# A decoder layer's mixer: sample columns taken with a pair's first 256, merged columns returned by DMA alone, two input tiles side by side

## The chip, the cores and the metric

The kernel runs on one core of a Trainium2 chip. The metric is the time of one execution on the device, in microseconds (us). Of three runs before the change the median is 3203.73 us, the lowest 3203.45 and the highest 3207.47. One execution was recorded by the profiler; it took 3211.86 us.

## The reference, cut to what matters

One layer works on 1024 prompt columns and 8 sample columns (each of 1024 channels), side by side in one array of NT = 1032 columns. The samples share every weight with the prompt but have states of their own.

```python
def _layer(h, ...):
    h = _layer_norm(DN_ALPHA * h + 0.5 * _swiglu(h, ...))
    mix, ... = _mixer(h, ...)
    h = _layer_norm(DN_ALPHA * h + mix)
    h = _layer_norm(DN_ALPHA * h + _xattn(h, ...))
    h = _layer_norm(DN_ALPHA * h + 0.5 * _swiglu(h, ...))

def _mixer(h, S0, shift0, h0, buf0, P):
    proj = h @ P['w_in']                      # RWKV columns, LRU, GeLU and two gates
    ...                                       # token shift, decay, keys
    S_new, y = _rwkv_scan(S0, r, decay, k, v, kk, a)
    rwkv_out = (group_norm(y) + bonus) * g
    ...                                       # causal convolution, gates, linear scan hs
    lru_out = hs * gelu(p_gelu)
    merged = gates[0] * rwkv_out + gates[1] * lru_out
    return merged @ P['w_mix_out'], ...
```

## The kernel before, in words

The layer is four stages: a feed-forward (`ffn`), the mixer, cross-attention, a second feed-forward. Activations lie transposed, 128 channels by columns, as a high and a low part (`HH`, `HL`, eight blocks of 128 channels each), and every large product is three matmuls (`mm3`, lines 125 to 127). This case is about the mixer alone, lines 543 to 1363.

In the mixer the 16 heads are eight pairs p, one for each block of 128 channels, and two pairs (p = 2g, 2g + 1) are worked together. The prompt is cut into n = 0 to 3 of 256 columns, so there are 16 units t = 4g + n. `NCW` (line 534) gives n = 3 eight columns more, the samples. The steps of a unit are Python generators:

- `stage` (line 808) loads a pair's projected columns from the DRAM tile `GD` (tiles `R` and `za`), makes keys, decays and scores, and stores the bonus. With n = 3 it also does the sample columns and keeps what the samples need in `P.sv` and `P.sg`; `samples_a` follows it.
- `inverse` (line 930) inverts 32 by 32 triangles on VectorE, 31 dependent steps over `tq` and `iv`, and sends the result through DRAM into `TT` and `TB`.
- `chain` (line 1081) carries the state over the four 64-column chunks of a unit and ends with the late steps `post` (line 1051), which normalise, gate and merge the two pairs' 256 columns into `ysb`.
- `branch` (line 985) is the linear recurrence of one pair and one n: it loads `cb` and `ge` from `GD`, works in `xc`, `gr`, `gi` and `lm`, and stores the result. With n = 3 it also does the samples' columns.
- `samples_b` (line 1153) is the samples' state update of one pair, on VectorE over tiles `ws` and `wt`; `samples_c` (line 1195) normalises and merges the samples' columns.
- `gemms` (line 660) is the stream of large products that fills TensorE: tiles of 128 output channels in three chunks of 344 columns (`CH3`), 24 matmuls a chunk, each tile's weights loaded in two halves one tile ahead (`load`, `split_half` at line 90; four halves have room). Its last tile is followed by `out_proj` (line 1238), 18 matmuls a chunk, over the merged columns of pairs 0 to 5.

Merged columns of pairs 0 to 5 go to the DRAM tile `MG` (lines 1075 and 1221). They may return into blocks 0 to 5 of `HH` and `HL` only when the last input tile has read a chunk there: `merged` (line 1226) loads 344 columns into an `ev` tile (line 1233), and `direct` (line 1046) copies them to `HH` on ScalarE and subtracts into `HL` on VectorE. The last two pairs merge into `HH` and `HL` at once, at `post`.

What sets the order: the program order gives priorities, and when the kernel is built a scheduler with estimated durations lays down each engine's own order from them; on the chip each engine follows it strictly. Loads and stores are all issued from SyncE's queue. The loop at line 1317 gives each unit its streams with a number of steps, and `rounds` (line 49) deals them out over 13 rounds, the fill by `FILL` (line 538). The streams of a unit t are:

```python
s = [(chain(units[t - 1], units[t]), 13)] if t else []
s.append((inverse(units[t]), 52))
if t + 1 < nu:
    s.append((stage_unit(t + 1), 40 if n == 2 else 34))
to = nu if t == nu - 1 else t
```

Branches up to unit `to` - 1 come next, then a pair's `samples_b` in units with n = 3 and n = 0, both pairs' `samples_c` in n = 1, and the fill. The last unit takes four branches, two `samples_b`, the rest of the fill and all late posts; the last two `samples_c` stand behind the loop (line 1338). Then the pools of the loop are given back (line 1339) and `out_last`, the first products of the next stage and the last `chain` run together.

## Time and profile before

| what | before |
|---|---|
| median of 3 runs | 3203.73 us (3203.45 to 3207.47) |
| profiled execution | 3211.86 us |
| span from the first to the last instruction | 3210.0 us |
| mean granted clock of TensorE | 0.969 |
| ScalarE (ACT) busy | 1432.5 us, 45% of the span |
| GpSimd (POOL) busy | 560.6 us, 17% |
| DMA | 386.72 MB in 381445 packets |

PE is TensorE, PEld its weight loads, DVE VectorE, SP SyncE. A granted clock of 1 stands for 2.4 GHz and 0.5 for 1.2 GHz; a mean between them is a share of time at each. The profiled execution lies 8.1 us above the median, so only differences within it are used. In the page's forty slices TensorE is at nine tenths or more through both feed-forwards; the slices around two thirds of the span, the mixer's end, are the low ones.

### The profile page before, as it was taken

What the parts mean: (1) busy time and instruction counts of PE and PEld (TensorE: products, weight loads), DVE (VectorE), ACT (ScalarE), POOL (GpSimd) and SP (SyncE); (2) the same over time, 40 slices, a digit from 0 to 9 for tenths busy, and PEclk for the clock granted to TensorE, in tenths of its full rate; (3) what the DMA queues carried; (4) which work ended last, traced back from release to release, by engine and by line L of the source; (5) the groups of instructions that cost most, each with busy time, mean ns of one, the idle gap of its engine ahead of it and who ended that gap; (6) DMA issues with size and microseconds to landing.
All of it is one profiled execution on the core that took longest, in us unless ns stands there. A gap on an engine that the chain in (4) does not pass through costs nothing. (4 is left out here: it accounts for less than half of the span.)

```text
span 3210.0 us, 63182 instructions
## 1 busy us (share of the span) xinstructions
PE 3018.8 (94%) x23324; PEld 2845.2 (89%) x23324; DVE 2202.1 (69%) x5895; ACT 1432.5 (45%) x3191; POOL 560.6 (17%) x526
## 2 busy tenths in 40 slices
PE   8999999999999999999998888789897999999997
PEld 8999999999888888888886777688887999999997
DVE  7666665574357888777877776776767666666556
ACT  5333352125565665655654554364235433334212
POOL 2222200132000101100110100350005322220111
PEclk9999999999999999999999979799999999999998
DMA  4222253314644455455544544654533222225321
GB/s 138 78 81 77 80 162 106 112 47 143 204 120 123 136 149 146 129 142 159 144 121 133 141 135 128 195 177 135 149 112 118 75 80 80 80 80 159 107 86 54
DMA packets 381445, 386.72 MB, mean 120 GB/s; under 512 B 144048, under 2 KB 282320, under 8 KB 381136
## 3 DMA queue, kind: packets, MB, share of 16 engines
q1 hardware_dynamic: 381136, 382.69, 40.1%
q8 instruction: 183, 3.00, 0.4%
q14 instruction: 126, 1.03, 0.1%
HBM read 277.54 MB, written 105.23 MB: 119 GB/s over the span
## 5 line engine op out<-in xcount | busy, mean ns | idle before, releaser
L125 PE MATMUL ps<-HH,wh 128*128 128x258 f32 (+1 forms) x2384 | 719.3, 302 | 17.0 <-ACT HH L510 7.9
L126 PE MATMUL ps<-HL,wh 128*128 128x258 f32 (+1 forms) x2384 | 717.4, 301 | 0.0
L127 PE MATMUL ps<-HH,wl 128*128 128x258 f32 (+1 forms) x2384 | 716.3, 301 | 0.0
L125 PE MATMUL g<-HH,wh 128*128 128x344 f32 (+2 forms) x1840 | 617.3, 336 | 17.3 <-ACT wh L99 6.5
L127 PE MATMUL g<-HH,wl 128*128 128x344 f32 (+2 forms) x1840 | 594.4, 325 | 3.2 <-DVE wl L100 3.1
L126 PE MATMUL g<-HL,wh 128*128 128x344 f32 (+2 forms) x1840 | 595.7, 324 | 0.3 <-POOL HL L215 0.2
L125 PEld LDWEIGHTS ps<-HH,wh 128*128 128x128 f32 x2384 | 452.1, 190 | 19.1 <-ACT HH L510 7.9
L126 PEld LDWEIGHTS ps<-HL,wh 128*128 128x128 f32 x2384 | 451.7, 189 | 0.5 <-DVE HL L511 0.4
L127 PEld LDWEIGHTS ps<-HH,wl 128*128 128x128 f32 x2384 | 451.0, 189 | 0.0
L125 PEld LDWEIGHTS g<-HH,wh 128*128 128x128 f32 x1840 | 355.2, 193 | 34.2 <-ACT wh L99 7.8
L127 PEld LDWEIGHTS g<-HH,wl 128*128 128x128 f32 x1840 | 354.1, 193 | 10.1 <-DVE wl L100 6.1
L126 PEld LDWEIGHTS g<-HL,wh 128*128 128x128 f32 x1840 | 355.8, 193 | 5.7 <-POOL HL L215 0.9
L228 ACT ACTIVATE wh<-raw 128x512 fp32r<-128x512 f32 x280 | 176.5, 631 | 321.8 <-PE ps L126 264.4
L334 POOL TENSOR_TENSOR raw<-raw 128x512 f32<-128x512 f32 x160 | 213.8, 1336 | 567.4 <-DVE wl L229 342.4
L229 DVE TENSOR_TENSOR wl<-raw,wh 128x512 fp32r<-128x512 f32 x280 | 206.5, 738 | 137.9 <-ACT wh L228 131.0
L100 DVE TENSOR_TENSOR wl<-raw,wh 128x512 fp32r<-128x512 f32 x302 | 218.7, 731 | 104.4 <-ACT wh L99 101.3
L99 ACT ACTIVATE wh<-raw 128x512 fp32r<-128x512 f32 x302 | 185.8, 627 | 219.3 <-PE ps L126 76.6
L442 DVE SCALAR_TENSOR_TENSOR acc<-ps,acc 128x344 f32<-128x344 f32 x336 | 168.9, 513 | 143.0 <-PE ps L127 142.0
L550 DVE TENSOR_TENSOR pr<-tq,iv 128x2 f32<-128x2 f32 (+30 forms) x496 | 161.0, 325 | 3.2
L555 ACT ACTIVATE ev<-g 128x344 f32<-128x344 f32 x192 | 87.3, 455 | 158.7 <-PE g L127 155.3
L945 DVE TENSOR_REDUCE tq<-pr 128x1 f32<-128x2 f32 (+30 forms) x496 | 121.9, 246 | 2.6
L374 ACT ACTIVATE g<-g 128x258 f32<-128x258 f32 x160 | 67.1, 419 | 114.0 <-DVE g L333 114.0
(410 smaller groups left out, 6364.4 us busy)
## 6 DMA issues: line engine op xcount, KB each, us to landing
raw<-in_wi_dram SPq DMA_DIRECT2D x176, 256.0 KB, 2.7
raw<-in_w_in_dram SPq DMA_DIRECT2D x116, 256.0 KB, 3.5
GD<-ev SPq DMA_DIRECT2D x168, 172.0 KB, 2.0
raw<-in_wo_dram SPq DMA_DIRECT2D x104, 256.0 KB, 3.4
raw<-HID SPq DMA_DIRECT2D x88, 258.0 KB, 3.2
HID<-g SPq DMA_DIRECT2D x80, 258.0 KB, 2.5
tg<-GD SPq DMA_DIRECT2D x32, 512.0 KB, 4.2
wt<-T SPq DMA_DIRECT2D x160, 64.0 KB, 2.7
```

Of the source, the lines that this page charges most:

```text
L99: nc.scalar.activation(out=hi, in_=raw, func=AF.Identity)
L100: S.low.tensor_tensor(out=lo, in0=raw, in1=hi.bitcast(F32), op=ALU.subtract)
L125: nc.tensor.matmul(ps, wh, xh, start=first, stop=False)
L126: nc.tensor.matmul(ps, wh, xl, start=False, stop=False)
L127: nc.tensor.matmul(ps, wl, xh, start=False, stop=last)
L228: nc.scalar.activation(out=hi, in_=x, func=AF.Identity)
L229: nc.vector.tensor_tensor(out=lo, in0=x, in1=hi.bitcast(F32), op=ALU.subtract)
L334: pool_tt = lambda o, a, b, op: nc.gpsimd.tensor_tensor(out=o, in0=a, in1=b, op=op)
L442: nc.vector.scalar_tensor_tensor(out=a, in0=q, scalar=0.5 / ALPHA, in1=a, op0=ALU.mult, op1=ALU.add)
L550: TTo = lambda o, a, b, op: nc.vector.tensor_tensor(out=o, in0=a, in1=b, op=op)
L555: ACT = lambda o, a, f=AF.Identity, **kw: nc.scalar.activation(out=o, in_=a, func=f, **kw)
L945: nc.vector.tensor_reduce(out=tq[:, 0:m, i], in_=pv, axis=mybir.AxisListType.X, op=ALU.add)
```

## The change

Sample columns move from a pair's last 256 columns (n = 3) to its first (n = 0): `stage` and `branch` load them as pieces of their own beside the 256, `samples_a` follows n = 0, `samples_b` comes in units n = 1 and 2, `samples_c` in n = 3. Branches are dealt out by halves of a unit, so that units 12 to 15 take two, three, three and two. Merged columns of pairs 0 to 5 are split into high and low part at `post` and at `samples_c`, stored into two DRAM tiles `MH` and `ML`, and return by two DMAs straight into `HH` and `HL`. The last two input tiles take turns by chunk, so that a chunk is free for the return when both have read it. Late posts of unit 14 run behind the loop. `ev` has two buffers where it had three at the end.

```diff
@@ mixer
+        MH, ML = (S.dram.tile([KT - 2, 128, NT], F32, name="M" + x) for x in "HL")
@@ project
-                e = pool.tile([128, 344], F32, tag="ev", name="ev", bufs=3 if then else 2)[:, :n]
+                e = pool.tile([128, 344], F32, tag="ev", name="ev", bufs=2)[:, :n]
@@ gemms
-            for j, (p, x, i) in enumerate(todo[:-1]):
+            for j, (p, x, i) in enumerate(todo[:-2]):
...
-            p, x, i = todo[-1]
             merges = []
-
-            def then(c0, n):
-                load(c0, n)
+            for c, (c0, n) in enumerate(CH3):
+                for j in (-2, -1):
+                    p, x, i = todo[j]
+                    if c - j == 2:
+                        load()
+                        load()
+                    for _ in project(p, *x, W[len(todo) + j], [(c0, n)], psg, t1):
+                        for m in merges:
+                            next(m, 0)
+                        yield
+                    if c == 2 and j == -2:
+                        load()
+                        load()
                 merges.append(merged(c0, n))
-
-            for _ in project(p, *x, W[len(todo) - 1], CH3, psg, t1, then):
-                for m in merges:
-                    next(m, 0)
-                yield
-            ready.update(((p, x[1]), "h"))
+            ready.update((p, x[1]) for p, x, i in todo[-2:])
+            ready.add("h")
@@ stage
-            c0, w = NCW[n]
+            c0, w = 256 * n, 256 if n else 264
...
             if n == 0:
                 nc.vector.memset(R[:, :, 0:1], 0.0)
-                nc.sync.dma_start(out=R[:, :, 1:1 + w], in_=GD[p][:, 0:3, 0:w])
+                nc.sync.dma_start(out=R[:, :, 1:257], in_=GD[p][:, 0:3, 0:256])
+                nc.sync.dma_start(out=R[:, :, 257:265], in_=GD[p][:, 0:3, NP:NT])
+                nc.sync.dma_start(out=za[:, :, 256:264], in_=GD[p][:, GZ:GA + 1, NP:NT])
...
-                if n == 3:
+                if n == 0:
                     STT(x[:, 256:264], shs[:, mt, :], mu[:, mt:mt + 1], x[:, 256:264], ALU.mult, ALU.add)
@@ branch
-                nc.sync.dma_start(out=cb[:, 3:3 + w], in_=GD[p][:, GL, 0:w])
+                nc.sync.dma_start(out=cb[:, 3:259], in_=GD[p][:, GL, 0:256])
+                nc.sync.dma_start(out=cb[:, 259:267], in_=GD[p][:, GL, NP:NT])
...
-            nc.sync.dma_start(out=ge, in_=GD[p][:, GE:G1 + 1, c0:c0 + w])
+            nc.sync.dma_start(out=ge[:, :, 0:256], in_=GD[p][:, GE:G1 + 1, c0:c0 + 256])
+            if n == 0:
+                nc.sync.dma_start(out=ge[:, :, 256:264], in_=GD[p][:, GE:G1 + 1, NP:NT])
...
-                nc.sync.dma_start(out=O["lru"][:, p, :], in_=P.hl)
+                nc.sync.dma_start(out=O["lru"][:, p, 1:9], in_=P.hl[:, 1:9])
...
+            if n == 3:
+                nc.sync.dma_start(out=O["lru"][:, p, 0:1], in_=P.hl)
@@ direct, now merge
-        def direct(k, c0, n, e):
-
-            ACT(S.HH[:, k, c0:c0 + n], e)
-            TTo(S.HL[:, k, c0:c0 + n], e, S.HH[:, k, c0:c0 + n].bitcast(F32), ALU.subtract)
+        def merge(k, c0, n, e, h, j):
+
+            if k >= S.npairs - 2:
+                assert "h" in ready
+                ACT(S.HH[:, k, c0:c0 + n], e)
+                TTo(S.HL[:, k, c0:c0 + n], e, S.HH[:, k, c0:c0 + n].bitcast(F32), ALU.subtract)
+                return
+            ACT(h.bitcast(F32R), e)
+            TTo(e.bitcast(F32R), e, h, ALU.subtract)
+            for to, x in ((MH, h), (ML, e)):
+                nc.sync.dma_start(out=to[k, :, c0:c0 + n], in_=x)
+            ready.add(("mg", k, j))
@@ post
-            if p < S.npairs - 2:
-                nc.sync.dma_start(out=MG[p, :, 256 * n:256 * n + 256], in_=ysb)
-                ready.add(("mg", p, n))
-            else:
-                assert "h" in ready
-                direct(p, 256 * n, 256, ysb)
+            merge(p, 256 * n, 256, ysb, sq, n)
@@ samples_c
-            while len(P.lm) < 4:
-                yield
+            assert P.lm and (p, G0) in ready
...
+            merge(p, NP, NS, y, v, 4)
@@ merged
-                e = tmp("ev", 344, 3)[:, :n]
-                nc.sync.dma_start(out=e, in_=MG[k, :, c0:c0 + n])
-                direct(k, c0, n, e)
+                for to, x in ((S.HH, MH), (S.HL, ML)):
+                    nc.sync.dma_start(out=to[:, k, c0:c0 + n].bitcast(F32), in_=x[k, :, c0:c0 + n])
@@ the loop
-                s.append((stage_unit(t + 1), 40 if n == 2 else 34))
-
-            to = nu if t == nu - 1 else t
+                s.append((stage_unit(t + 1), 40 if n == 3 else 34))
+
+            to = 2 * t + min(2, max(0, t - nu + 4))
             if to > nbr:
-                s.append((branches(range(nbr, to)), 12 * (to - nbr)))
+                s.append((branches(range(nbr, to)), 6 * (to - nbr)))
                 nbr = to

-            if t == nu - 1:
-                s.append((pairs_of(samples_b, g), 25))
-            elif n == 3 or (n == 0 and t):
-                p = (t - 1) // 2 if n == 0 else 2 * g
-                s.append((samples_b(p, Ps[p]), 13))
-            if n == 1 and g:
-                s.append((pairs_of(samples_c, g - 1), 10))
+            if n in (1, 2):
+                s.append((samples_b(2 * g + n - 1, Ps[2 * g + n - 1]), 13))
+            if n == 3:
+                s.append((pairs_of(samples_c, g), 10))
             s.append((part(fill, FILL[t]) if t < nu - 1 else fill, FILL[t]))
-            rounds(13, s, late_steps, t < nu - 1)
-        weave(pairs_of(samples_c, S.npairs // 2 - 1))
+            rounds(13, s, late_steps, True)
         actx.close()
...
-        weave((chain(units[-1], None), 45), (early(), 43), (part(mem, 35), 20))
+        weave((chain(units[-1], None), 45), *((g, 20) for g in late_steps), (early(), 43), (part(mem, 35), 20))
```

In `branches` the index now counts single branches: pair `2 * (j // 8) + j % 2`, columns `j // 2 % 4`. The other places where `n == 3` stood for the sample columns in `stage` and `branch` read `n == 0` in the same way.

## Rows read from the trace of the kernel before

**Rows 1.** The page, busy time of each engine: us, share of the span, instructions.
```profile
PE 3018.8 (94%) x23324; PEld 2845.2 (89%) x23324; DVE 2202.1 (69%) x5895; ACT 1432.5 (45%) x3191; POOL 560.6 (17%) x526
```

**Rows 2.** Instructions of tile `iv`: duration ns min/median/max, first and last start.
```profile
L936 SPq DMA_DIRECT2D iv<-D x64: 303/420/2007, 904.4 to 1949.3; - x64
```

**Rows 3.** Windows: length, then PE, PEld, DVE, ACT, POOL busy; clock, DMA share, GB/s.
```profile
1579.10:1640.70 61.60, 60.13 (x535) 53.27 (x531) 50.56 (x187) 36.62 (x87) 8.40 (x8) 1.00 0.50 143
...
1712.10:1789.20 77.10, 64.56 (x507) 52.35 (x508) 56.29 (x195) 38.09 (x83) 5.38 (x6) 0.91 0.47 127
1789.20:1867.60 78.40, 67.10 (x563) 56.96 (x561) 57.95 (x200) 45.33 (x111) 10.37 (x9) 0.89 0.50 142
1867.60:1947.90 80.30, 73.64 (x530) 64.47 (x529) 55.53 (x191) 44.04 (x108) 10.14 (x7) 0.85 0.47 134
1947.90:2003.00 55.10, 47.85 (x391) 41.65 (x391) 43.40 (x151) 23.81 (x48) 2.02 (x2) 0.91 0.53 144
2003.00:2031.00 28.00, 11.37 (x65) 7.53 (x66) 17.52 (x52) 13.89 (x27) 1.05 (x1) 0.57 0.60 162
2031.00:2150.00 119.00, 103.84 (x818) 94.31 (x819) 88.77 (x201) 58.92 (x146) 64.54 (x77) 0.90 0.65 198
```

**Rows 4.** Windows of ten microseconds behind the loop, the same columns.
```profile
2030.00:2040.00 10.00, 7.85 (x31) 6.41 (x31) 5.71 (x22) 3.07 (x9) 4.79 (x3) 0.50 0.66 211
2040.00:2050.00 10.00, 7.93 (x67) 6.54 (x67) 8.07 (x21) 2.88 (x7) 3.68 (x4) 0.59 0.61 178
```

**Rows 5.** Waits from 1948 to 2050 us: us in total, times, longest.
```profile
PE m L1013 <- DVE xc L551: 10.7, 1, 10.7
ACT xc L555 <- DMA cb<-GD: 9.0, 1, 9.0
```

**Rows 6.** Windows for tile `wt` alone (`samples_b`): DVE busy, clock, DMA share, GB/s.
```profile
1712.10:1789.20 77.10, 7.76 (x19) 0.91 0.47 127
...
1947.90:2031.00 83.10, 15.00 (x36) 0.80 0.55 150
```

**Rows 7.** Windows for tile `xc` alone (`branch`): PE, PEld, DVE, ACT busy.
```profile
1867.60:1947.90 80.30, 2.45 (x8) 1.34 (x8) 4.64 (x10) 2.01 (x4) 0.85 0.47 134
```

**Rows 8.** Windows for tile `lm` alone (`branch`): DVE busy.
```profile
1867.60:1947.90 80.30, 3.45 (x8) 0.85 0.47 134
```

**Rows 9.** Windows for tile `tq` alone (`inverse`): DVE busy.
```profile
1947.90:2031.00 83.10, 17.46 (x62) 0.80 0.55 150
```

**Rows 10.** Instructions of tile `ev` from 1828 to 1900 us (`merged`, `direct`).
```profile
L1233 SPq DMA_DIRECT2D ev<-MG x18: 319/353/430, 1830.7 to 1893.3; - x18
L555 ACT ACTIVATE HH<-ev x18: 473/480/491, 1835.3 to 1898.4; 128x344 fp32r<-128x344 f32 x18
L550 DVE TENSOR_TENSOR HL<-ev,HH x18: 500/510/519, 1841.6 to 1898.9; 128x344 fp32r<-128x344 f32 x18
```

**Rows 11.** Instructions of tile `ysb` (`post`) from 1948 to 2031 us.
```profile
L555 ACT ACTIVATE HH<-ysb x3: 409/417/418, 1957.5 to 2024.9; 128x256 fp32r<-128x256 f32 x3
L550 DVE TENSOR_TENSOR HL<-ysb,HH x3: 418/419/425, 1958.0 to 2026.1; 128x256 fp32r<-128x256 f32 x3
```

**Rows 12.** DMA issues by line: count, KB each, median us from issue to landing.
```profile
R<-GD SPq DMA_DIRECT2D x8, 397.5 KB, 3.8
...
MG<-ysb SPq DMA_DIRECT2D x24, 128.0 KB, 1.9
...
e<-GD SPq DMA_DIRECT2D x8, 4.0 KB, 2.6
```

**Rows 13.** The page, costliest groups: a weight half's split into two parts.
```profile
L100 DVE TENSOR_TENSOR wl<-raw,wh 128x512 fp32r<-128x512 f32 x302 | 218.7, 731 | 104.4 <-ACT wh L99 101.3
L99 ACT ACTIVATE wh<-raw 128x512 fp32r<-128x512 f32 x302 | 185.8, 627 | 219.3 <-PE ps L126 76.6
```

**Rows 14.** A window of the first feed-forward, where every matmul has 344 columns.
```profile
480.00:560.00 80.00, 80.00 (x508) 80.00 (x507) 44.60 (x80) 19.55 (x38) 5.16 (x4) 1.00 0.36 109
```

**Rows 15.** Waits of SP's queue from 1789.2 to 1867.6 us.
```profile
SPq L643 <- ACT ep L555: 16.1, 2, 15.9
```

More of the change, by code (lines that the diff above doesn't have):

```diff
@@ L540, with mixer @@
 LATE = ("ev", "ref", "dend", "scl", "sm", "wsb", "sf", "ysb", "gsq", "ivc", "lm")
-def mixer(octx, S, I, O, MG, HD, pre):
+def mixer(octx, S, I, O, HD, pre):
     nc, tc = S.nc, S.tc
@@ L811, in stage @@
             col = lambda t: t[:, p:p + 1]
-            c0, w = NCW[n]
+            c0, w = 256 * n, 256 if n else 264
             assert all((p, j) in ready for j in range(3))
             R = ta.tile([128, 3, 265], F32, tag="R", name="R", bufs=1)
+            za = ta.tile([128, 2, 264], F32, tag="za", name="za", bufs=1)
             if n == 0:
                 nc.vector.memset(R[:, :, 0:1], 0.0)
-                nc.sync.dma_start(out=R[:, :, 1:1 + w], in_=GD[p][:, 0:3, 0:w])
-            else:
-                nc.sync.dma_start(out=R[:, :, 0:1 + w], in_=GD[p][:, 0:3, c0 - 1:c0 + w])
-            za = ta.tile([128, 2, 264], F32, tag="za", name="za", bufs=1)
-            nc.sync.dma_start(out=za[:, :, :w], in_=GD[p][:, GZ:GA + 1, c0:c0 + w])
+                nc.sync.dma_start(out=R[:, :, 1:257], in_=GD[p][:, 0:3, 0:256])
+                nc.sync.dma_start(out=R[:, :, 257:265], in_=GD[p][:, 0:3, NP:NT])
+                nc.sync.dma_start(out=za[:, :, 256:264], in_=GD[p][:, GZ:GA + 1, NP:NT])
+            else:
+                nc.sync.dma_start(out=R[:, :, 0:257], in_=GD[p][:, 0:3, c0 - 1:c0 + 256])
+            nc.sync.dma_start(out=za[:, :, 0:256], in_=GD[p][:, GZ:GA + 1, c0:c0 + 256])
             xs = []
@@ L859, in stage @@
             nc.sync.dma_start(out=GD[p][:, GB, c0:c0 + 256], in_=bv)
-            if n == 3:
+            if n == 0:
                 TTo(P.sg[:, 0, :], xv[:, 256:264], pb[:, 256:264], ALU.mult)
@@ L871, in stage @@
             nc.vector.tensor_copy(out=dend[:, 4 * n:4 * n + 4], in_=cs3[:, :, 63])
-            if n == 3:
+            if n == 0:
                 for j, t in ((0, xr), (2, xk), (5, xv)):
@@ L987, in branch @@
             col = lambda t: t[:, p:p + 1]
-            c0, w = NCW[n]
+            c0, w = 256 * n, 256 if n else 264
             while (p, G1) not in ready:
@@ L997, in branch @@
                 nc.vector.memset(cb[:, 0:3], 0.0)
-                nc.sync.dma_start(out=cb[:, 3:3 + w], in_=GD[p][:, GL, 0:w])
+                nc.sync.dma_start(out=cb[:, 3:259], in_=GD[p][:, GL, 0:256])
+                nc.sync.dma_start(out=cb[:, 259:267], in_=GD[p][:, GL, NP:NT])
             else:
-                nc.sync.dma_start(out=cb[:, 0:3 + w], in_=GD[p][:, GL, c0 - 3:c0 + w])
+                nc.sync.dma_start(out=cb[:, 0:259], in_=GD[p][:, GL, c0 - 3:c0 + 256])
             ge = ta.tile([128, 2, 264], F32, tag="ge", name="ge")[:, :, :w]
-            nc.sync.dma_start(out=ge, in_=GD[p][:, GE:G1 + 1, c0:c0 + w])
+            nc.sync.dma_start(out=ge[:, :, 0:256], in_=GD[p][:, GE:G1 + 1, c0:c0 + 256])
+            if n == 0:
+                nc.sync.dma_start(out=ge[:, :, 256:264], in_=GD[p][:, GE:G1 + 1, NP:NT])
             xc = tmp("xc")[:, :w]
@@ L1006, in branch @@
                 STT(xc[:, 0:256], cb[:, j:j + 256], col(V["cw%d" % j]), xc[:, 0:256], ALU.mult, ALU.add)
-                if n == 3:
+                if n == 0:
                     STT(xc[:, 256:264], cst[:, p, j, :], col(V["cw%d" % j]), xc[:, 256:264], ALU.mult, ALU.add)
@@ L1029, in branch @@
             P.hl = tmp("hl", 9, 4)
-            if n == 3:
+            if n == 0:
                 TTo(hs[:, 256:264], gr[:, 256:264], lst[:, p, :], ALU.mult)
@@ L1219, in samples_c @@
             STT(y, sg[:, 2, :], 0.5, y, ALU.mult, ALU.add)
-            if p < S.npairs - 2:
-                nc.sync.dma_start(out=MG[p, :, NP:NT], in_=y)
-                ready.add(("mg", p, 4))
-            else:
-                direct(p, NP, NS, y)
+            merge(p, NP, NS, y, v, 4)
         def merged(c0, n):
@@ L1246, in out_proj @@
                     load(c0, n)
-                    e = tmp("ev", 344, 3)[:, :n]
+                    e = tmp("ev", 344, 2)[:, :n]
                     ACT(e, q, scale=1.0 / ALPHA)
@@ L1292, in stage_unit, with branches @@
                 yield from stage(U, i)
-            for i in range(2 if n == 3 else 0):
+            for i in range(0 if n else 2):
                 yield from samples_a(U.p0 + i, Ps[U.p0 + i])
-        def branches(ts):
-            for t in ts:
-                for i in range(2):
-                    p = 2 * (t // 4) + i
-                    yield from branch(p, t % 4, Ps[p])
+        def branches(js):
+            for j in js:
+                p = 2 * (j // 8) + j % 2
+                yield from branch(p, j // 2 % 4, Ps[p])
         def part(g, n):
@@ L1315, in mixer @@
         fill = gemms()
-        rounds(13, [(stage_unit(0), 34), (part(fill, 42), 42)], late_steps, True)
+        rounds(13, [(stage_unit(0), 40), (part(fill, 42), 42)], late_steps, True)
         for t in range(nu):
@@ L1613 @@
     nc = S.nc
-    MG = S.dram.tile([8, 128, NT], F32, name="MG")
     HD = S.dram.tile([8, 128, NT], F32, name="HD")
@@ L1624 @@
               [(itertools.chain(*x[1:]), 64)], keep=HD, after=I["w_in"][24])
-    pre = mixer(ctx, S, I, O, MG, HD, pre)
+    pre = mixer(ctx, S, I, O, HD, pre)
     pre = attention(S, I, 2, pre, I["wi2"][0], H2)
```

5 lines of the change are left out of this document (2 added, 3 removed).

## The prediction

> **What bounds the kernel now.** I read first the page's engine table: PE is busy for nearly all of the span [rows 1], so a gain can only come from a stretch in which PE waits or runs at the lower clock. The windows by unit show where. A unit is one turn of the mixer's loop, 256 columns of two pairs; I cut the windows where the sixteen units load `iv`, four loads each [rows 2], and count units 0 to 15 with n = unit modulo 4. Unit 10 keeps PE busy 60.13 of 61.6 us at full clock; units 12, 13 and 14 leave 12.5, 11.3 and 6.7 us idle, at a clock of 0.91 to 0.85; unit 15 is the poor one [rows 3]. Its last 28 us, from 2003 to 2031, hold 65 matmuls: PE is busy 11.37 us of it, at a mean clock of 0.57, and two of the next ten-microsecond slices still run near half rate [rows 3, 4].
>
> The waits there say why: PE stands 10.7 us in order behind the gate matmul of a branch, which needs `xc` from DVE, which needs ACT, which waits 9.0 us for the load of `cb` [rows 5]. Unit 15 is where the loop puts all its leftovers: four branches one after the other instead of two, two `samples_b` instead of none, the drain of the late posts, and behind the loop a `samples_c` alone. When the out-projection's matmuls run out, only these are left, and the pools that the next stage needs are not free until they end.
>
> **The change part by part**, against the profiled execution (3211.86 us, span 3210.0); it lies 8.1 us over the median 3203.73, so a difference found in it is taken off the median.
>
> **The tail (lines 1293 to 1338).** The sample columns ride on n = 0 instead of n = 3, so a pair's `samples_b` come in units n = 1 and 2 and `samples_c` in n = 3; the branches of the last units are pulled forward to two, three, three, two in units 12 to 15, where they were two, two, two, four. Unit 15 thus loses two `samples_b`, 15.0 us of DVE (36 instructions) [rows 6], and two branches. A branch costs DVE half of the five `xc` operations' 4.64 us and half of the `lm` operations' 3.45 us for two branches, and one more `gi` operation of about 0.42, so 4.5 us [rows 7, 8]. Of 60.9 us of DVE work in unit 15 (43.40 + 17.52 [rows 3]) 24 go. What is late next is that unit's inverse: 62 operations, 17.46 us [rows 9]; even at two thirds of DVE it is done some 26 us after it starts, well inside the 55 us in which PE is still fed. So the stretch from 2003 to 2031 shrinks to what its 65 matmuls take at full clock, 11.37 x 0.57 = 6.5 us: **-21.5**. In 2030 to 2050 PE is busy 7.85 and 7.93 us at 0.50 and 0.59 [rows 4]; at full clock 8.6 instead of 15.8. The weights of the next stage still have to come, so I take half of the 7.2: **-3.5**. Ends: -39 (all 28, and the 7.2 with the 4.2 idle) and -15 (a third of it stays with the two branches left).
>
> **Unit 12** loses a `samples_b`, 7.76 us of DVE [rows 6], and has 12.5 us of idle PE. Most of those gaps are shared with other waits: **-3** (ends -7.8 and 0).
>
> **Units 13 and 14** each gain a `samples_b` (7.5) and a branch (4.5). They lose the return of the merged columns: 18 ACT copies of 480 ns and 18 DVE subtractions of 510 ns [rows 10], between 1830 and 1899, that is 4.6 us of DVE and 4.3 of ACT each (the `samples_c` that leave unit 13 are not counted). DVE becomes 57.95 + 7.4 = 65.4 of 78.4 us and 55.53 + 7.4 = 62.9 of 80.3, 83 and 78%. Unit 10 ran PE at 98% with DVE at 82% (50.56 of 61.6) [rows 3], so this fits: **+2** (ends 0 and +15, if all comes on top).
>
> **The split at the posts.** The ACT copy and the DVE subtraction now happen in `post`, 417 and 419 ns [rows 11], 24 times, mostly in units where PE is the bound: **0**; all exposed it would be 24 x 0.42 = +10. `gsq` is now held until its store has landed, 1.9 us [rows 12], where only `ysb` was; the next post waits for `ysb` that long already.
>
> **The last two input tiles side by side.** Four halves of weights is all the room there is, so tile 49 loads when tile 47 is through, one chunk (24 matmuls) ahead of use, and the first out-projection tile when tile 48 has read its last chunk. An uncovered half costs an ACT copy of 627 and a DVE subtraction of 731 ns [rows 13]; a bound is four of them, 5.4 us: **+2** (low end 0, as the raw halves arrive ahead). One out-projection chunk is 18 matmuls or about 2.8 us (508 matmuls of this width in 80 us [rows 14]); two chunks cover the store of the one before, so two `ev` buffers do: 0.
>
> **Posts left over.** The two posts of unit 14 now run behind the loop: seven DVE operations each, at the 419 ns of one of them [rows 11] 5.9 us in all, in a stretch where DVE is at 88.77 of 119 us [rows 3]: **+2** (ends 0 and +6).
>
> **DMA.** Some 88 issues more: 40 sample pieces and last-column stores, 30 second halves of merged stores, 18 second loads. At 0.32 to 0.43 us of the queue each (the old loads, [rows 10]) that is about 30 us spread over the mixer's 1100: 0. The sample pieces go beside a larger load: 2.6 us to landing for 4 KB, 3.8 for 397.5 KB [rows 12]; issued at most 0.4 later each, a piece lands no later than the large one: 0, upper bound 2.6 once per pair, +21. The Trainium skill (DMA: Bandwidth & Descriptors, Rules for kernel authors) speaks against this part: coalesce small transfers, since below 64 KB one pays mostly overhead; by that rule, with each pair's first stage late by one piece, the sum would lose nearly all its gain. The rows bear the rule out as to the overhead (2.6 us for 4 KB) but show it beside a longer load.
>
> **Sum:** -25 - 3 + 2 + 0 + 2 + 2 = **-22**, that is 3190 in the profiled execution and **3182** against the median.
>
> **The rivals.**
> *The clock comes back too* (about -46, **3158**). With the merged columns off ACT and DVE, units 12 to 14 could run at full clock: 64.56, 67.10 and 73.64 us of busy PE at 0.91, 0.89 and 0.85 would shrink by 24 in all. For: those dips lie around the merge stretch. Against: their DVE load rises.
> *Slower: DVE becomes the bound of the n = 2 units* (**3212**). Units 2, 6 and 10 had no sample work and now get 7.5 us of it and two posts' subtractions: unit 10 has 50.56 + 7.5 + 0.8 = 58.9 of 61.6 us. To stand at the 82% it had it needs 71.8, +10.2; three such units are +31, against -22: +9. It decides from some 7 us per unit. For: the neighbours that lose the work are PE-bound and give nothing back. Against: the sample work is not urgent until n = 3, and matmuls held up can fill later idle time (unit 12).
> *The gain is eaten on SP* (**3203**). The 36 loads into HH and HL wait for PE's last read of a chunk, in SP's order; behind them stand weight loads, stores of FD, and the loads of `iv` and `TT` on which the inverse waits. SP has already stood 15.9 us behind ACT once in unit 13 [rows 15]; three chunks at 7 us would be +21. For: it is in order. Against: the old loads waited there too.
> That the change does not do what it says has no room: the moved work is written into the loop.
>
> **How the numbers follow.** A measurement of this kernel can tell about 0.2%, 6.4 us, from no change. Forecast 0.63 (its own range 3168 to 3196), clock 0.12, DVE 0.14, SP 0.11. Faster: 0.63 + 0.12 + 0.03 from the edges of the other two = 0.78; the same: 0.08 of SP and 0.03 of DVE = 0.11; slower: 0.10 of DVE and 0.01 of SP = 0.11. The range from 3158 to 3208 takes in the SP case and leaves out most of the DVE case and half of the clock case.
>
> **What would show it.** Right: from the last unit's `iv` loads to the first matmuls behind the loop 55 to 62 us instead of 83; no wait of PE on `xc` near 10 us; `wt` work on DVE at about 7.8 in n = 1 and 2 and none in unit 15; clock above 0.9 there. Wrong: n = 2 units beyond 68 us with PE idle (DVE); SP waits of several us at the new loads into HH (SP); a gap of PE before tile 49's chunks (weights); units 13 and 14 beyond 85 us.

## The result and the profile after

The change made the kernel slower: 3232.09 us (median of 4 runs, 3226.65 to 3233.93) against 3203.72 (3203.45 to 3207.47), a ratio of 1.0083 with a 95% interval from 1.0066 to 1.0100. The forecast was 3182, its range 3158 to 3208. Against the profiled execution of before (span 3210.0) that of after has a span of 3232.1 us.

The page of after, busy time of each engine (us, share of the span, instructions), answers to [rows 1]:

```profile
PE 3041.1 (94%) x23324; PEld 2866.4 (89%) x23324; DVE 2200.5 (68%) x5907; ACT 1438.1 (44%) x3209; POOL 557.3 (17%) x526
```

PE works 22 us longer on the same 23324 matmuls, about as much as the whole span grew (22.1). DVE is no busier than before. The mean granted clock is 0.961 where it was 0.969, so the first thing to look for is time at the lower clock.

**Where the time went.** I cut the trace of the changed kernel (after) where the sixteen units load `iv`, as for [rows 2]. In the windows (length; PE, PEld, DVE, ACT, POOL busy; granted clock; DMA share; GB/s) the units 12, 13, 14, the first part of unit 15 and the stretch behind the loop answer to [rows 3]; ahead of them stands one window over units 0 to 11:

```profile
900.30:1753.80 853.50, 803.22 (x6677) 713.42 (x6677) 643.92 (x2224) 492.06 (x1132) 85.72 (x82) 0.95 0.49 137
1753.80:1815.10 61.30, 60.43 (x529) 52.79 (x523) 51.11 (x171) 39.69 (x90) 6.57 (x7) 1.00 0.55 156
1815.10:1897.30 82.20, 65.10 (x481) 54.50 (x479) 57.51 (x193) 35.90 (x84) 5.55 (x6) 0.83 0.59 168
1897.30:1992.00 94.70, 81.26 (x590) 70.28 (x591) 65.83 (x204) 52.33 (x119) 5.20 (x6) 0.79 0.52 151
1992.00:2031.00 39.00, 37.38 (x340) 33.86 (x340) 30.04 (x121) 19.69 (x42) 4.25 (x3) 1.00 0.47 137
2031.00:2060.00 29.00, 18.54 (x131) 14.46 (x126) 13.74 (x35) 8.96 (x21) 2.01 (x2) 0.54 0.33 89
```

The same window over units 0 to 11 of before:

```profile
904.40:1712.10 807.70, 769.09 (x6620) 684.04 (x6619) 623.07 (x2141) 472.75 (x1084) 79.00 (x78) 0.99 0.50 137
```

The reader sees two things that pull against each other. Unit 12 begins at 1753.8 instead of 1712.1, 41.7 us late: the loss lies in units 0 to 11, to which the forecast's sum gave nothing. From unit 12 to the end 19.6 of it come back (3232.1 - 3210.0 - 41.7); against the medians, 28.4 us apart, it would be 13, since the profiled execution of before lay above its median.

The 45.8 us by which the first window is longer divide like this. PE idles 50.3 us of it (853.50 - 803.22) against 38.6: **+11.7**. The granted clock, added up from the trace's record of it, is at its lower level (1.2 GHz) for 81.9 us against 23.8. PE is busy in 76.2 of them against 21.0, and work at half rate takes twice its time, so half of the 55.2 more is lost: **+27.6**. The remaining 6.5 go with the 57 more matmuls in the window: work that is done earlier and comes back later. So most of the loss is clock.

**Where the clock falls.** In units 0 to 11 of before, 6 stretches at the lower clock begin; in after 11. Every one of the 11 begins in a gap of PE or within 3.6 us behind one, and these gaps are short, 0.2 to 4.6 us. Two of them, as windows of after: the ten microseconds or so ahead of the fall, the stretch at half rate, and for the first what follows.

```profile
1386.60:1398.60 12.00, 9.10 (x86) 8.31 (x84) 7.07 (x35) 4.61 (x13) 0.00 (x0) 1.00 0.23 73
1398.60:1408.80 10.20, 8.68 (x36) 7.19 (x33) 6.80 (x32) 4.14 (x12) 1.09 (x2) 0.50 0.50 150
1408.80:1418.80 10.00, 9.69 (x77) 8.48 (x76) 9.91 (x41) 8.45 (x21) 2.37 (x2) 1.00 0.46 118
1436.00:1446.40 10.40, 8.62 (x92) 7.33 (x92) 8.20 (x29) 8.53 (x19) 2.25 (x2) 1.00 0.35 94
1446.40:1460.10 13.70, 13.70 (x71) 12.09 (x70) 4.64 (x15) 7.50 (x21) 1.87 (x1) 0.50 0.27 73
```

The waits of PE in after from 1390 to 1400 and from 1440 to 1448 us (total, times, longest):

```profile
PE m L800 <- ACT s L555: 2.5, 1, 2.5
...
PE sc L920 <- DVE SC L550: 0.9, 1, 0.9
PE m L1164 <- DVE sv L551: 0.9, 1, 0.9
```

Two waits of 0.9 us stand ahead of 13.7 us at half rate in which PE has no gap at all: 1.8 us of waiting, 6.9 us of clock. The Trainium skill (TensorE: Matmul & The Clock Gate, "A second HAM failure mode: psum-queue depth-cycling") tells of the like in another kernel, of bf16 matmuls that cycle through the banks of PSUM: PE idles briefly between groups of matmuls, often enough that its clock swings between two levels. The trace agrees as to the short idles and the swing; that PSUM is behind it here no run shows. The number of short gaps does not decide it: gaps of at least 0.8 us number 18 in units 0 to 11 of before and 19 in after; the stretches at half rate number 6 and 11.

**The new tail.** From the last unit's `iv` loads to the first matmul of the next stage 53.8 us pass (1992.0 to 2045.8) where it was 83.4. Up to 2031 unit 15 keeps PE busy 96% of the time, at full clock. What is late next is in the windows of tile `tq` (`inverse`; DVE busy) and in two waits of the stretch from 1992 to 2060 us:

```profile
1992.00:2031.00 39.00, 14.95 (x57) 1.00 0.47 137
2031.00:2060.00 29.00, 2.61 (x6) 0.54 0.33 89
```

```profile
PEld y L1084 <- ACT ysb L555: 4.5, 2, 3.9
...
ACT TT L555 <- PE m L984: 4.2, 1, 4.2
```

Six operations of the last inverse are still to end at 2031, then its trip through DRAM, and the last chain begins only at 2056. PE has little else: 18.54 us busy of 29, at 0.54. The ten-microsecond windows that answer to [rows 4] are worse than before from 2040 on:

```profile
2030.00:2040.00 10.00, 6.63 (x66) 4.88 (x64) 7.57 (x23) 3.54 (x7) 0.57 (x1) 0.67 0.32 90
2040.00:2050.00 10.00, 5.18 (x22) 4.17 (x22) 3.92 (x10) 2.15 (x5) 0.51 (x2) 0.50 0.41 102
```

The next stage's first matmul is 14.5 us late, the end of the kernel 22.1: of the 27 us regained up to that matmul 7.6 are lost again behind it.

### The profile page after: what moved, and what is told of

Read it like the earlier page. It is cut to its first block, busy times and chain, and to the rows that moved or that the text cites. A ratio compares the mean times of both kernels' runs of the same rounds, so it can differ in the third digit from the quotient of the medians.

```text
span 3232.1 us, 63343 instructions
## 1 busy us (share of the span) xinstructions
PE 3041.1 (94%) x23324; PEld 2866.4 (89%) x23324; DVE 2200.5 (68%) x5907; ACT 1438.1 (44%) x3209; POOL 557.3 (17%) x526
## 5 line engine op out<-in xcount | busy, mean ns | idle before, releaser
L125 PE MATMUL g<-HH,wh 128*128 128x344 f32 (+2 forms) x1840 | 628.0, 342 | 21.2 <-ACT ev L555 6.0
L126 PE MATMUL g<-HL,wh 128*128 128x344 f32 (+2 forms) x1840 | 602.6, 328 | 0.5 <-POOL HL L215 0.2
L125 PEld LDWEIGHTS g<-HH,wh 128*128 128x128 f32 x1840 | 359.7, 196 | 40.3 <-ACT ev L555 8.4
L100 DVE TENSOR_TENSOR wl<-raw,wh 128x512 fp32r<-128x512 f32 x302 | 218.3, 731 | 95.6 <-ACT wh L99 93.4
```

Source lines behind the costliest of these rows:

```text
L100: S.low.tensor_tensor(out=lo, in0=raw, in1=hi.bitcast(F32), op=ALU.subtract)
L125: nc.tensor.matmul(ps, wh, xh, start=first, stop=False)
L126: nc.tensor.matmul(ps, wh, xl, start=False, stop=False)
```

## The experiments

All ratios are to the kernel before on the same chip, with 95% intervals (before took 3203.7 to 3211.4 us on the chips used, so absolute times are not compared across them). Beside them stand, from each trace, how late unit 12 begins (before: 1712.1), and for units 0 to 11 how long PE idles (window less busy time) and how long the clock is at 1.2 GHz.

| kernel | ratio [interval] | unit 12 late, us | PE idle, us | at 1.2 GHz, us |
|---|---|---|---|---|
| before | 1 | 0 | 38.6 | 23.8 |
| after | 1.0083 [1.0066, 1.0100] | +41.7 | 50.3 | 81.9 |
| u_samples | 1.0098 [1.0082, 1.0115] | +14.4 | 48.8 | 36.9 |
| u_merge | 0.9998 [0.9984, 1.0012] | +16.8 | 47.7 | 40.8 |
| u_serial | 1.0073 [1.0051, 1.0095] | +43.7 | 50.6 | 88.3 |
| u_branches | 1.0124 [1.0099, 1.0148] | +37.4 | 51.6 | 64.9 |
| own_buffer | 1.0087 [1.0060, 1.0115] | +49.4 | 51.5 | 95.6 |
| no_split | 1.0091 [1.0061, 1.0121] | +40.5 | 56.4 | 61.4 |
| split_pool | 1.0081 [1.0055, 1.0107] | +40.3 | 55.7 | 57.0 |
| only_split | 1.0062 [1.0031, 1.0093] | +21.4 | 43.8 | 44.3 |
| second_store | 1.0070 [1.0050, 1.0091] | +23.8 | 45.1 | 57.8 |
| store_act | 1.0032 [1.0016, 1.0047] | +10.8 | 44.0 | 41.1 |
| only_branches | 1.0000 [0.9987, 1.0013] | -2.4 | 38.1 | 20.4 |
| u_both | 1.0047 [1.0030, 1.0064] | +20.1 | 45.1 | 67.5 |
| p_tiny | 1.0100 [1.0083, 1.0118] | +26.2 | 44.7 | 61.2 |
| p_stage | 0.9992 [0.9980, 1.0005] | -8.2 | 39.3 | 17.0 |
| p_swap | 1.0027 [1.0017, 1.0037] | +15.3 | 43.5 | 40.9 |
| p_sb | 1.0038 [1.0025, 1.0051] | +14.9 | 46.8 | 27.2 |
| a_stage | 1.0051 [1.0036, 1.0066] | +31.3 | 51.2 | 54.4 |
| m_stage | 0.9945 [0.9928, 0.9963] | +4.9 | 37.7 | 44.2 |

The last three columns come from one execution each. How far they can be trusted is shown by kernels that follow the same order up to unit 12, on VectorE, ScalarE and SyncE to the instruction: u_serial and u_branches follow after's, only_branches before's. Their unit 12 starts at +43.7, +37.4 and +41.7, and at -2.4 and 0; their time at 1.2 GHz is 88.3, 64.9 and 81.9, and 20.4 and 23.8. So the same order gives the same start to about 6 us, and differences of some 20 us at 1.2 GHz between late kernels say little.

### Undoing one part at a time

**u_samples**: in the first three groups the sample work goes back to its old units.

```diff
-            if n in (1, 2):
+            if g == 3 and n in (1, 2):
...
-            if n == 3:
+            elif (g < 3 and n == 3) or (n == 0 and t):
+                p = (t - 1) // 2 if n == 0 else 2 * g
+                s.append((samples_b(p, Ps[p]), 13))
+            if n == 1 and g:
+                s.append((pairs_of(samples_c, g - 1), 10))
+            if t == nu - 1:
```

> The changed kernel with samples_b and samples_c of the first three groups put back to the units they had before (n = 3, the next n = 0, the next n = 1); the last group and everything else as changed. Theory A (sample work in units n = 1 and 2 stretches units n = 2 and 3): unit 12, which starts 41.7 us later after the change than before (1753.8 against 1712.1), starts at 1710 to 1725 again, and the time falls by 20 to 35 us to 3197 to 3212. Rival B (the split of merged columns in post, two ACT copies and two DVE subtractions a unit, stretches them): unit 12 stays beyond 1740 and the time within 6 us of 3232.

Neither A nor B came out. Unit 12 begins 27 us earlier than in after, nearly where A had it, yet the time stays: unit 13, with the old work beside the new, takes 96.5 us instead of 82.2, and PE idles 25.8 us in it.

**u_merge**: one store and the return through `ev`, as before.

```diff
...
-            ACT(h.bitcast(F32R), e)
-            TTo(e.bitcast(F32R), e, h, ALU.subtract)
-            for to, x in ((MH, h), (ML, e)):
-                nc.sync.dma_start(out=to[k, :, c0:c0 + n], in_=x)
+            nc.sync.dma_start(out=MH[k, :, c0:c0 + n], in_=e)
...
-                for to, x in ((S.HH, MH), (S.HL, ML)):
-                    nc.sync.dma_start(out=to[:, k, c0:c0 + n].bitcast(F32), in_=x[k, :, c0:c0 + n])
+                e = tmp("ev", 344, 2)[:, :n]
+                nc.sync.dma_start(out=e, in_=MH[k, :, c0:c0 + n])
+                ACT(S.HH[:, k, c0:c0 + n], e)
+                TTo(S.HL[:, k, c0:c0 + n], e, S.HH[:, k, c0:c0 + n].bitcast(F32), ALU.subtract)
```

> The changed kernel with merged columns stored once and returned through an ev tile, an ACT copy and a DVE subtraction as before; the rest as changed. Theory A: unit 12 still starts beyond 1740, the time is 3226 to 3240, a little worse, since 18 copies and subtractions come back into units 13 and 14. Rival B: unit 12 starts 15 to 40 us earlier than 1753.8, the time falls to 3200 to 3218.

The whole loss is gone with this part: 0.9998. Unit 12 is still 16.8 us late and the tail makes up for it. So the way of the merged columns, costed at 0 before unit 12, is the first suspect.

**u_serial**: the last two tiles one after the other.

```diff
...
-            for c, (c0, n) in enumerate(CH3):
-                for j in (-2, -1):
...
+            for _ in project(p, *x, W[len(todo) - 1], CH3, psg, t1, then):
...
```

> The changed kernel with the last two input tiles one after the other again. Both A and B: unit 12 starts within 5 us of 1753.8, since these tiles come in unit 13; the time within 8 us of 3232. Rival C (the side-by-side tiles starve for weights and hold SP): 10 us or more come back, all of them behind the start of unit 13.

1.0073 beside 1.0083: no difference that these intervals can tell. That is in keeping with the +2 forecast for the side-by-side tiles.

**u_branches**: branches and late posts as before.

```diff
-            to = 2 * t + min(2, max(0, t - nu + 4))
+            to = 2 * (nu if t == nu - 1 else t)
...
-            rounds(13, s, late_steps, True)
+            rounds(13, s, late_steps, t < nu - 1)
...
```

> The changed kernel with the branches of the last units dealt out as before (two, two, two, four) and the late posts drained inside the loop. A and B: unit 12 starts within 5 us of 1753.8; unit 15 and the start of the next stage come 10 to 20 us later, the time is 3240 to 3250. Rival D (pulling branches forward and late posts behind the loop is what costs): the time falls by 8 us or more.

Some 13 us slower than after by the ratios (1.0124 against 1.0083): beside the other parts, this one helps.

### What in the merged columns' way costs it

**own_buffer**: the high part in a buffer of its own instead of `gsq`.

```diff
-            merge(p, 256 * n, 256, ysb, sq, n)
+            merge(p, 256 * n, 256, ysb, tmp("mh", 256, 1, t1), n)
```

> The changed kernel with a buffer of its own for the high part in post, instead of gsq, so that gsq comes free without waiting for a store. Theory B2 (the split costs because gsq and ysb are held until two stores have landed, which delays the next post): the time falls by 12 to 28 us to 3204 to 3220. B1 (the ACT and DVE operations themselves) and B3 (twice as many stores in SP's order): within 7 us of 3232.

1.0087, where theory B2 had 12 to 28 us less: holding `gsq` until its store has landed is not the cause.

**no_split**: no copy, no subtraction; the same columns are stored twice.

```diff
-            ACT(h.bitcast(F32R), e)
-            TTo(e.bitcast(F32R), e, h, ALU.subtract)
-            for to, x in ((MH, h), (ML, e)):
+            for to, x in ((MH, e), (ML, e)):
```

> The changed kernel without the copy and the subtraction in post and in samples_c for pairs 0 to 5; the unsplit columns are stored twice, so that stores and loads are as changed, and the two parts that the out-projection reads are not the high and the low part. B1: the time falls to 3200 to 3214, as without the split. B2 and B3: within 8 us of 3232, since all DMAs and their waits stay.

1.0091: the 24 operations on each engine are not the cause either.

**split_pool**: the subtraction on POOL.

```diff
-            TTo(e.bitcast(F32R), e, h, ALU.subtract)
+            (nc.gpsimd if n > NS else nc.vector).tensor_tensor(out=e.bitcast(F32R), in0=e, in1=h, op=ALU.subtract)
```

> The changed kernel with the subtraction in post on POOL instead of DVE for pairs 0 to 5. B1 with DVE as the bound: the time falls by 10 to 25 us, to 3207 to 3222. B2 and B3: within 8 us of 3232, or above, since POOL is slower and the store comes later.

1.0081, the same again.

**only_split**: the kernel before with the split at the posts, two stores and the return by DMA (the `merge` of the change's diff), nothing else of the change.

> The kernel before with the split in post, two stores and the return by DMA alone; samples, branches and the last input tiles as before. If the split costs by itself (its waits or stores): 3222 to 3240. If it costs only together with sample work in n = 1 and 2, where DVE is full: 3200 to 3214, since 18 copies and subtractions go from units 13 and 14.

1.0062, unit 12 21.4 us late. Alone, too, this part loses time in units to which only the posts' work was added.

**second_store** and **store_act**: the kernel before with one more store of `ysb` per post, to a DRAM tile that nobody reads, from SP's queue (shown) or ACT's.

```diff
...
+                nc.sync.dma_start(out=MX[p, :, 256 * n:256 * n + 256], in_=ysb)
```

> The kernel before with each post of pairs 0 to 5 storing its merged columns a second time, to a place that nobody reads: 24 stores of 128 KB more on SP, nothing else. Theory E (a second store in SP's order, holding ysb longer, is what the split costs; the kernel before with the split alone started unit 12 21 us later): unit 12 starts at 1725 to 1740, the time rises by 8 to 25 us to 3215 to 3235. Rival F (the stores are free; the order of instructions that the scheduler lays down is what differs): within 6 us of the kernel before, or any sign.

> The same with the second store issued from ACT's queue, so that SP issues what it did before. E with SP's queue as the place: within 6 us of the kernel before. E with ysb held as the place: the time rises as in the run before it, by 8 to 25 us, and somewhat more, since ACT waits for ysb. Rival F: no relation between the two.

24 stores that do nothing cost 0.70% on SP's queue and 0.32% on ACT's. The first is as much as only_split (0.62%): the second store can stand for the whole part. second_store alone is what theory E had forecast; store_act, some 10 us slower than before, fits neither of E's two places.

**p_tiny**: the same with 8 of the 256 columns, 4 KB instead of 128.

```diff
...
+                nc.sync.dma_start(out=MX[p, :, 256 * n:256 * n + 8], in_=ysb[:, 0:8])
```

> The kernel before with the second store of second_store cut to 8 columns (4 KB for 128 KB), every engine in the same order as there. If the transfers cost (DMA engines shared with the other loads): within 6 us of the kernel before. If the issue, the hold of ysb or the order costs: within 7 us of second_store's 3238.

1.0100: the transfer is not the cause. The waits on it are small, too. In units 0 to 11 the trace of p_tiny names one engine that waits for this store, 0.4 us, the last of these lines (total, times, longest); the others are two waits of PE:

```profile
PE y L1116 <- DVE QZ L1110: 7.3, 6, 3.3
...
PE m L969 <- DVE TN L967: 2.7, 2, 1.5
...
ACT ysb L555 <- DMA MX<-ysb: 0.4, 1, 0.4
```

The first of them in before, units 0 to 11 (its L1114 is L1116 there); the second is not among PE's waits there:

```profile
PE y L1114 <- DVE QZ L1108: 2.9, 5, 1.2
```

`QZ` and `TN` have nothing to do with `ysb`. Nor do loads come late behind the added issues: the waits of all engines on DMAs in units 0 to 11 add up to 20.2 us in p_tiny, 19.9 in second_store and 19.9 in before. What changed is the instructions' place: in p_tiny 25% of VectorE's 2141 instructions in units 0 to 11 (told apart by line, operation and tiles) stand outside the longest order that its trace has in common with that of before; second_store and p_tiny follow one order, to the instruction. In store_act it is 13%, in only_branches none. And again half-rate stretches follow short waits; one in p_tiny, as windows, with the wait ahead of it:

```profile
1534.40:1544.40 10.00, 8.51 (x78) 7.76 (x76) 3.22 (x17) 3.34 (x8) 0.00 (x0) 1.00 0.53 169
1544.40:1551.20 6.80, 5.91 (x29) 5.08 (x30) 5.11 (x21) 2.86 (x8) 1.19 (x1) 0.50 0.09 28
```

```profile
PE m L795 <- ACT s L555: 1.8, 1, 1.8
```

The window over units 0 to 11 of p_tiny is 24.4 us longer than that of before:

```profile
906.20:1738.30 832.10, 787.41 (x6627) 700.69 (x6625) 624.09 (x2141) 469.06 (x1083) 80.22 (x78) 0.96 0.48 133
```

PE idles 44.7 us, +6.1, and the clock is down for 61.2 us, with PE busy in 55.1 of them against 21.0, which costs 17.1: 23.2 together.

### The other parts alone

**only_branches**: the kernel before with branches by halves (two, three, three, two at the end) and late posts behind the loop.

```diff
...
-            to = nu if t == nu - 1 else t
+            to = 2 * t + min(2, max(0, t - nu + 4))
...
```

> The kernel before with only its last branches pulled forward (two, three, three, two in units 12 to 15) and the late posts of unit 14 behind the loop; samples and merged columns as before. Forecast of the prediction for this part: unit 15 loses two branches' 9 us of DVE and the wait on the last branch; 8 to 16 us faster, 3190 to 3198, with units 0 to 11 unchanged to 5 us. Rival: the two samples_b left in unit 15 set its end and the gain is under 4 us.

1.0000, as the rival had it. From the last unit's loads to the next stage's first matmul 84.6 us pass: the two `samples_b` left there run until 2029.3, that matmul starts at 2030.4. With the samples moved and the branches left (u_branches) it is 60.5 us, with both moved 53.8.

**u_both**: u_merge and u_samples together; of the change there remain the sample columns riding on n = 0, the last group's new units, branches and tiles.

> The changed kernel with merged columns returned through an ev tile as before and with the first three groups' sample work in its old units: what is left of the change is sample columns at n = 0, the last group's sample work in units 13 and 14, side-by-side tiles, branches and late posts. If both costs add up (17 us for sample work, 25 for the split, both before unit 12): unit 12 starts at 1705 to 1718 and the time is 3180 to 3200. If units 12 and 13, which then hold the sample work of two groups, eat it as they did with the split: 3205 to 3220.

1.0047, which neither forecast had: unit 12 is 20.1 us late, although both suspects are out of units 0 to 11 and of the change only the sample columns at n = 0 are left there. The parts do not add up: u_samples +14.4, u_merge +16.8, without both +20.1, with both +41.7. That speaks against a price per part; whether it speaks for the order the next runs had to tell.

### How much order alone is worth

**p_stage**, **p_swap** and **p_sb**: the kernel before with the same instructions dealt out a little differently: a stage counted as 36 or 42 steps for 34 or 40; a unit's two posts in the other order; a `samples_b` counted as 11 steps for 13.

```diff
-                s.append((stage_unit(t + 1), 40 if n == 2 else 34))
+                s.append((stage_unit(t + 1), 42 if n == 2 else 36))
```

```diff
-            yield itertools.chain(*(post(U.p0 + i, n, Y[:, 256 * i:256 * i + 256]) for i in range(2))), 14
+            yield itertools.chain(*(post(U.p0 + i, n, Y[:, 256 * i:256 * i + 256]) for i in (1, 0))), 14
```

```diff
-                s.append((samples_b(p, Ps[p]), 13))
+                s.append((samples_b(p, Ps[p]), 11))
```

> The kernel before with two steps more in the number by which the stage stream is dealt out over the rounds (36 and 42 for 34 and 40): no instruction added or left out, about a quarter of VectorE's and a sixth of SyncE's instructions at other places in their order. Theory F (the order alone moves the time by as much as the change did): 8 us or more away from the kernel before, most likely slower. E (second stores cost by issue or hold): within 6 us of it.

> The kernel before with the two posts of a unit in the other order, second pair first: the same instructions, over a quarter of VectorE's at other places. F: 8 us or more away from the kernel before, most likely slower. E: within 6 us.

> The kernel before with samples_b dealt out as 11 steps in place of 13: the same instructions, over a quarter of VectorE's at other places, a tenth of SyncE's. F: 8 us or more away from the kernel before, most likely slower. E: within 6 us.

With no work added the time goes from 0.9992 to 1.0038 and the start of unit 12 from -8.2 to +15.3 us; 26 to 32% of VectorE's instructions are out of the common order. p_swap and p_sb meet theory F's 8 us or more; p_stage, 2.5 us faster, does not. Order alone is thus worth about half of what a second store seemed to cost, but none of the three reaches 1.0070 or 1.0100. Nor does the displaced share rank the losses: p_stage with 26% loses nothing, p_tiny with 25% loses 1.0%.

**a_stage** and **m_stage**: the same other count of a stage, in after and in u_merge.

```diff
-                s.append((stage_unit(t + 1), 40 if n == 3 else 34))
+                s.append((stage_unit(t + 1), 42 if n == 3 else 36))
```

> The kernel after with a unit's stage dealt as 36 or 42 steps for 34 or 40: the same instructions in another order. Theory (what the change loses before unit 12 is lost through the order that the scheduler lays down, and with the same work another order may or may not lose it): the time moves by more than 6 us from the kernel after, to 3205 to 3225 us, and the start of unit 12 moves with it (41.7 us late in the kernel after). Rival (the additional work and stores cost it in whatever order): within 6 us of the kernel after, about 3232 us, unit 12 still 35 to 45 us late.

> The kernel after with the merged columns stored once and returned as before (as in the run u_merge), and a unit's stage dealt as 36 or 42 steps for 34 or 40: u_merge's instructions in another order. Theory (order alone moves some 10 us either way): 3198 to 3220 us; at the low end it beats the kernel before by 0.3%. Rival (u_merge's 17 us at the start of unit 12 belong to the samples' place in units n = 1 and 2, whatever the order): within 4 us of the kernel before, unit 12 starting 13 to 20 us late.

Both move by more than the rivals allowed (a_stage by the ratios, some 10 us; its 3227.64 us were taken on a chip where before took 3211.42), and m_stage further down than the theory's 3198: a_stage from 1.0083 to 1.0051, unit 12 10.4 us earlier; m_stage from 0.9998 to 0.9945, unit 12 11.9 us earlier. In a_stage PE idles as long as in after (51.2 and 50.3 us); the clock is down for 54.4 us instead of 81.9, and half of these 27.5 us is about the difference; the lowest of the three traces in after's order has 64.9. The windows over units 0 to 11, first a_stage, then m_stage:

```profile
902.10:1743.40 841.30, 790.08 (x6647) 699.87 (x6648) 641.61 (x2222) 484.74 (x1124) 84.55 (x82) 0.97 0.50 139
```

```profile
900.30:1717.00 816.70, 779.08 (x6634) 696.21 (x6633) 633.16 (x2196) 476.12 (x1095) 89.86 (x82) 0.97 0.51 140
```

But 31.3 us of after's delay stay in a_stage, so this other order wins back only a quarter of it. m_stage is 0.55% faster than before (3194.94 us beside 3211.42 in the same runs): the samples' move, the branches and the side-by-side tiles, with the merged columns returned as they were and a stage counted as 36 or 42 steps, beat both kernels; with the old count (u_merge) they did not. From unit 12 to the end its trace gains 20.4 us on that of before (span 3194.5, so -15.5, of which +4.9 stand before unit 12).

## Why the prediction was wrong

**The tail: right in place, and the near size of the sum is luck.** PE's wait on `xc` near 10 us [rows 5] is gone, unit 15 has no `wt` work, its clock is 1.00, and 53.8 us lie between its loads and the next stage (forecast 55 to 62). The sum from unit 12 on was -22; after shows -19.6, of which some 6 are the matmuls done earlier, and m_stage -20.4. Its terms do not come out so near: in after unit 12 gives -15.8 where -3 was forecast, units 13 and 14 +18.2 for +2, unit 15 up to the next stage's first matmul -29.6 for -21.5, and what follows +7.6. The -3.5 for the clock behind the loop became +7.6 together with the +2 of the left-over posts: the prediction had named the inverse as late next and gave it 26 us, but its 62 operations end at 2034.3, 42 us after its loads and 33 us after their own start, and the last chain waits for them. The 26 us came from DVE's busy time alone [rows 9]; in the trace of before the same operations, each of which needs the one before it, already took 36.6 us (1957.7 to 1994.3). And PE was fed not for 55 us but for 39. In only_branches and u_branches the branches gain nothing alone and some 7 us beside the samples' move (60.5 to 53.8).

**Units 12 to 14.** Unit 12 lost its idle PE (0.9 us instead of 12.5). Units 13 and 14 take 177 us instead of 158.7, +18 where +2 (at most +15) was forecast, and unit 14's 94.7 is beyond the 85 us named as a sign of being wrong; PE idles 30.5 us in them instead of 18.0, and the clock is 0.83 and 0.79. DVE is busy for only 70% of both, where the forecast had 83 and 78%, so it is not the sum of its load that binds there; which wait does is open. Over the three units it is +2.5, forecast -1.

**The step that failed** is the zero that the sum gave units 0 to 11, which start unit 12 41.7 us late. The term that stood for them is the split at the posts, put at 0 because it comes "mostly in units where PE is the bound", with +10 as what it would be all exposed. The work is hidden, as it said: without the copy and the subtraction (no_split) nothing is won. But 24 second stores that hardly anyone waits for (0.4 and 0.7 us) cost 0.7 to 1.0% alone, 22 to 32 us, more than the +10 of the bound. That bound counted instructions and not what the scheduler lays down around them. The sample work had no term for these units at all, and it is as large there: with it put back unit 12 starts 27.3 us earlier (u_samples), with the merged columns put back 24.9 (u_merge), and with both put back 20.1 us of delay are still left. The DMA term fell with it: 88 issues at 0.4 us, "0", were costed by what the queue is busy, not by the new order. The store's own time and its size are excluded by p_tiny, late loads behind it by the unchanged waits on DMAs, the buffer by own_buffer, the arithmetic by no_split and split_pool. That the order is the cause is argued by elimination and not shown by a run that has this order without the stores, or the stores without this order; that another order of the same instructions moves the time by up to 12 us one way (p_sb) and 17 us the other (m_stage) is shown. Why orders with the second store on SP lose more than the three other orders tried is open: u_both, without it, is no better up to unit 12 than u_samples with it.

**The rivals.** The DVE rival came closest. The units n = 2 of the first three groups take 68.8, 70.6 and 76.5 us instead of 62.1, 63.8 and 61.6: +28 where it said +31, and beyond the 68 us named as its sign. They shrink to 195 us in sum in u_samples, from 216. The last of them in after and in u_samples:

```profile
1599.20:1675.70 76.50, 66.79 (x552) 57.81 (x553) 57.58 (x188) 38.72 (x88) 6.09 (x6) 0.91 0.48 134
```

```profile
1589.50:1651.90 62.40, 59.30 (x536) 53.65 (x530) 53.25 (x183) 40.07 (x94) 5.04 (x6) 1.00 0.58 160
```

Its mechanism is not confirmed: in after DVE has 75% of that unit, less than the 82% at which PE idled only 1.5 us in unit 10 of before [rows 3], and what PE waits for longest in it is a weight half:

```profile
PE g L125 <- ACT wh L99: 5.0, 2, 4.6
```

Its claim that the neighbours give nothing back fails: the units n = 0 of the first three groups take 10 us less in after than before, and in u_merge the units n = 3 do. Its price stood on 3 of 12 units; n = 1 and n = 3 grew by 14 and 13 us in after as well. The clock rival had the right quantity and the wrong sign: the clock decided, and went down. SP's longest wait in unit 13 is 9.7 us, less than the 15.9 of [rows 15], and none of its longest waits in units 12 to 15 is at the new loads, so that rival did not come. The DMA rule of the Trainium skill (DMA: Bandwidth & Descriptors, Rules for kernel authors) was weighed for the sample pieces. Here the waits of all engines on DMAs in units 0 to 11 of after came to 24 us against 20, none of them PE's; m_stage, which keeps all the sample pieces, starts unit 12 only 4.9 us late, where the rule's case was +21; and a store of 4 KB cost no less than one of 128 KB. Overhead of small transfers is not what the runs show as the loss.

## What to carry to other kernels

Where a scheduler lays down each engine's order, an added instruction that is hidden and hardly waited for can still redraw the order of the rest, so run the same instructions in a few other orders first: their spread (here 0.9992 to 1.0038) is the least that a part must move before it has a price, and the best of them may be the better kernel (m_stage). Undo parts one at a time and in pairs; where the results do not add up, a part has no price of its own. For an engine that is 94% busy, read its idle time and its clock over the long even stretch too, not only where the profile shows holes: short waits there can cost several times their length.

## What had not been expected

- A 4 KB store, 24 times, whose landing was waited for once, 0.4 us, made the kernel 1.0% slower.
- Waits of PE of 0.2 to 4.6 us are followed by 3.4 to 13.7 us at 1.2 GHz, some of them and not others: with 18, 19 and 17 gaps of at least 0.8 us, before, after and p_tiny fall to the lower clock 6, 11 and 12 times in units 0 to 11.
- Dealing out the same steps in other counts moved the kernel with u_merge's instructions by 0.5%, some 17 us, nearly what the new tail regains.
